# Value and gate columns in one product, second-layer weights split once, and more convolution taps on ScalarE and GpSimd, in a two-layer gated-linear-attention and convolution trunk

## The chip, the cores and the metric

The kernel runs on one core of one Trainium2 chip. The metric is device microseconds of one launch. TensorE (PE) multiplies, VectorE (DVE), ScalarE (ACT) and GpSimd (POOL) work element by element, and SyncE (SP) issues every DMA of this kernel. The language is a tile framework: the program says what is computed in which tile, a scheduler orders the instructions of each engine by priority (by default the order of the program) on a simulated time line, and it hands out buffers and semaphores. An instruction moved ahead with `high_priority(offset=n)` is treated as if it stood n instructions earlier.

## The reference, cut to what matters

The input x has 2048 tokens of 1024 channels. All arithmetic is float32.

```python
h = rmsnorm(x, norm_w[0])                       # layer 0: gated linear attention, 4 heads
q, k, v, z, g_lr = split(h @ gla_w_in)          # 512, 512, 1024, 1024, 16 columns
log_a = log_sigmoid(g_lr @ w_g2 + b_g) / 16
o = gla_chunked(q * 128**-0.5, k, v, log_a)     # chunks of 64 tokens, a state per head runs over chunks
o = o * rsqrt(mean(o * o) + EPS) * gn_w         # per head of 256 value columns
x = x + (o * silu(z)) @ gla_w_out

h = rmsnorm(x, norm_w[1])                       # layer 1: convolution module
a, gl, z = split(h @ conv_w_in)                 # 1024 columns each
u = causal_depthwise_conv(a * sigmoid(gl), dw_w, 31 taps) + dw_b
u = silu(layernorm(u, ln_w, ln_b))
x = x + (u * silu(z)) @ conv_w_out
out = rmsnorm(x, final_norm_w)
```

## The kernel before, in words

**Products.** TensorE works in float32r, a rounded form. To keep float32's accuracy every operand is split into a high part (the rounded copy) and a low part (the rest), and each product is three matmuls: high by high, high by low, low by high (`mm3`, L139 to L145). The splitting is one copy on ScalarE and one subtraction on VectorE or GpSimd for each tile.

**Weights.** All weights lie in DRAM as 32 units of 1 MB (`wall`): 1024 rows by 256 columns, as 128 partitions by 8 row blocks. Units 0 to 11 are the heads of the first layer (for each head: query and key columns, value columns, z columns), 12 to 15 its output projection, 16 to 23 and 24 to 27 the second layer's input (a with gl, and z), 28 to 31 its output. `order` lists the units as they are used; the 4 output units of the second layer come four times, and every other unit twice, once for each half of the tokens. `load_unit` (L110 to L130) brings a unit in two parts of 512 KB through two raw buffers `wr`; for each part ScalarE writes `wh` (L124) and GpSimd writes `wl` (L125; VectorE for the first two units). Two units are kept, the one in use and the next.

**Layer 0.** The tokens go in two halves of 1024, each as two blocks of 512. For each head, `qk` makes query and key for a block feature-major (128 weight columns against 512 tokens, `proj_f`); `values` makes the value rows, 128 tokens at a time against 256 columns of weights (`proj_t`); then `head` goes over the 8 token tiles: the z columns of a tile (again `proj_t` with 256 columns), and the three stages of `core` (scores, mixing with the state, turning), which are issued one token tile apart. In head 0 the values are put into the banks `pb`, so that they can be made while query and key of the block wait in the banks `mm` for the decay factors of `gate`. The output projection `out1` goes over pairs of units; under each pair over both blocks; under each block over 4 channel tiles. After the first block of the second pair it starts the next half (`ahead`: `start_block` with its loads of x, `prep_x`, and the gate's low-rank product `gate_low`, whose small weights `wgs` stay in a tile of their own).

**Layer 1.** `in2` goes over the 12 input units of each half in the order of `SCHED`. A unit of kind u gives one channel tile of a times sigmoid(gl) (`glu`), and its convolution is queued as background work (`bg`): even and odd outputs come from three chains of 16, 15 and 16 taps on VectorE (L634 to L642), of which the first taps of two chains go to ScalarE (products, L620 and L622) and GpSimd (sums, L624); `SIDES` says how many, for each half and channel tile. `pump` issues background work after each piece of TensorE's work. Three `u` tiles are there, so a channel tile waits for the convolution three tiles before it. `layernorm` follows as background work, then `out2`, the output projection, the residual sum and the last normalisation (sum of squares on VectorE, L851).

## Time and profile before

| | us |
|---|---|
| median of 3 runs | 1691.66 (1691.0 to 1695.15) |
| span of the profiled execution, first to last instruction | 1691.3 |
| TensorE busy in it | 1617.2 |
| VectorE busy | 1015.6 |
| GpSimd busy | 936.0 |
| ScalarE busy | 742.2 |

The span and the median differ by 0.4 us, so that the sum over the profile can be read as the time. A busy time is the time in which at least one instruction of the engine runs; matmuls overlap one another, so TensorE is counted busy for a short while after its last one has started.

### The profile page before, as it was taken

How to read it: one execution, taken by the hardware profiler on the slowest of the kernel's cores; microseconds unless marked ns; L12 is line 12 of the kernel's file. 1: busy time of each engine (PE TensorE's matmuls, PEld its weight loads, DVE VectorE, ACT ScalarE, POOL GpSimd, SP SyncE). 2: the span in 40 equal slices, each digit the busy share in tenths (PEclk: the TensorE clock that was granted, in tenths of full speed). 3: DMA queues.
4: the chain of work that ended last, by engine and by line, in shares of the span. 5: the costliest groups of instructions: out<-in, count | busy, mean ns of one | idle time of the engine just before them, and what ended most of it. 6: DMA issues, size and time to landing. Idle time of an engine off the chain costs nothing.

```text
span 1691.3 us, 23564 instructions
## 1 busy us (share of the span) xinstructions
PE 1617.2 (96%) x9028; PEld 1413.4 (84%) x9028; DVE 1015.6 (60%) x1473; ACT 742.2 (44%) x1254; POOL 936.0 (55%) x795
## 2 busy tenths in 40 slices
PE   8999999999999999999999999998999999997887
PEld 6989998988889999999888887876777778776687
DVE  7423232342334323226153999989799999987865
ACT  6645252343466444325232544544462554434432
POOL 4444343334745342424433999983788997465553
PEclk9999999999999999999999999999999999998998
DMA  5021111244511121204461111225127122632743
GB/s 188 30 78 57 63 51 57 76 130 139 164 34 55 58 72 42 75 33 132 132 196 46 63 50 57 85 80 154 38 69 238 61 68 94 206 125 88 235 176 124
DMA packets 74015, 165.68 MB, mean 98 GB/s; under 512 B 7760, under 2 KB 16464, under 8 KB 73904
## 3 DMA queue, kind: packets, MB, share of 16 engines
q1 hardware_dynamic: 73904, 164.19, 29.9%
q8 instruction: 70, 1.15, 0.3%
q14 instruction: 41, 0.34, 0.1%
HBM read 128.51 MB, written 35.65 MB: 97 GB/s over the span
## 4 chain that ended last, share of the span: by engine, by line
PE 62%; DVE 16%; POOL 7%; DMA 6%; issue 4%; ACT 3%; SPq 0%; POOLq 0%; DVEq 0%; ACTq 0%
PE mm L144 52%; DVE pb L638 6%; PE pb L144 3%; DVE al L190 2%; DMA wr<-in_wall_dram 2%; PE pb L388 1%; POOL wl L125 1%; PE pb L390 1%; POOL convB L624 1%; DVE S L713 1%; PE pm L379 1%; POOL convA L624 1%; DVE d L734 1%; POOL b L736 1%; DVE pb L642 1%
## 5 line engine op out<-in xcount | busy, mean ns | idle before, releaser
L144 PE MATMUL mm<-ah,wh 128*128 128x512 f32 (+1 forms) x1600 | 599.1, 389 | 43.2 <-DVE u L761 10.7
L144 PE MATMUL mm<-al,wh 128*128 128x512 f32 (+1 forms) x1600 | 594.6, 387 | 1.7 <-DVE al L190 1.7
L144 PE MATMUL mm<-ah,wl 128*128 128x512 f32 (+1 forms) x1600 | 592.9, 387 | 2.3 <-POOL wl L125 2.3
L125 POOL TENSOR_TENSOR wl<-wr,wh 128x1024 fp32r<-128x1024 f32 x140 | 358.5, 2575 | 195.2 <-ACT wh L124 190.3
L144 PEld LDWEIGHTS mm<-ah,wh 128*128 128x128 f32 x1600 | 304.0, 191 | 109.0 <-DVE u L761 13.1
L144 PEld LDWEIGHTS mm<-ah,wl 128*128 128x128 f32 x1600 | 303.3, 191 | 62.4 <-POOL wl L125 4.2
L144 PEld LDWEIGHTS mm<-al,wh 128*128 128x128 f32 x1600 | 303.9, 191 | 59.7 <-DVE al L190 2.6
L144 PE MATMUL mm<-wh,ah 128*128 128x256 f32 x896 | 259.2, 289 | 0.0
L144 PE MATMUL mm<-wh,al 128*128 128x256 f32 x896 | 254.6, 284 | 0.0
L144 PE MATMUL mm<-wl,ah 128*128 128x256 f32 x896 | 254.2, 284 | 0.0
L124 ACT ACTIVATE wh<-wr 128x1024 fp32r<-128x1024 f32 x144 | 145.3, 1050 | 109.0 <-PE mm L144 78.9
L638 DVE SCALAR_TENSOR_TENSOR pb<-u,C,pb 128x512 f32<-128x512 f32 x252 | 183.8, 747 | 0.5
L638 DVE SCALAR_TENSOR_TENSOR pb<-u,dwc,pb 128x512 f32<-128x512 f32 x240 | 179.4, 748 | 1.6
L144 PEld LDWEIGHTS mm<-wl,ah 128*128 128x128 f32 x896 | 171.4, 191 | 0.4
L144 PEld LDWEIGHTS mm<-wh,ah 128*128 128x128 f32 x896 | 171.3, 191 | 0.4
L144 PEld LDWEIGHTS mm<-wh,al 128*128 128x128 f32 x896 | 171.3, 191 | 0.0
L622 ACT ACTIVATE prod<-u,C 128x512 f32<-128x512 f32 x148 | 105.6, 721 | 137.6 <-POOL convA L624 78.5
L624 POOL TENSOR_TENSOR convA<-convA,prod 128x512 f32<-128x512 f32 x74 | 99.5, 1344 | 6.6 <-ACT prod L622 3.0
L624 POOL TENSOR_TENSOR convB<-convB,prod 128x512 f32<-128x512 f32 x74 | 99.6, 1346 | 3.9 <-ACT convB L620 0.7
L397 DVE SCALAR_TENSOR_TENSOR S<-S,dec,pb 128x256 f32<-128x256 f32 x56 | 26.8, 479 | 95.4 <-PE pb L144 95.3
L401 POOL TENSOR_TENSOR ss<-ss,e 128x1 f32<-128x1 f32 x64 | 13.3, 208 | 124.5 <-ACT g L400 124.5
L523 DVE TENSOR_TENSOR Q<-mm,Q 128x512 f32<-128x512 f32 x32 | 22.0, 688 | 92.7 <-PE mm L144 78.9
(205 smaller groups left out, 2245.3 us busy)
## 6 DMA issues: line engine op xcount, KB each, us to landing
wr<-in_wall_dram SPq DMA_DIRECT2D x144, 512.0 KB, 4.1
raw<-in_xT_dram SPq DMA_DIRECT2D x32, 256.0 KB, 3.8
Q<-in_xT_dram SPq DMA_DIRECT2D x32, 256.0 KB, 3.2
x_scratch<-Q SPq DMA_DIRECT2D x32, 256.0 KB, 3.2
sz_scratch<-t SPq DMA_DIRECT2D x32, 256.0 KB, 2.3
b<-sz_scratch SPq DMA_DIRECT2D x32, 256.0 KB, 3.8
g_scratch<-st SPq DMA_DIRECT2D x48, 128.0 KB, 1.9
raw<-g_scratch SPq DMA_DIRECT2D x24, 256.0 KB, 3.7
```

The costliest lines, as they stand in the source:

```text
L124: act.activation(wh[:, ks, :], raw, AF.Copy)
L125: (dve if i < 2 else pool).tensor_tensor(wl[:, ks, :], raw, wh[:, ks, :].bitcast(F32), ALU.subtract)
L144: pe.matmul(ps, s, m, start=(i == 0), stop=(i == 3 * n - 1))
L190: dve.tensor_tensor(lo, src, hi.bitcast(F32), ALU.subtract)
L379: pe.matmul(s_ps[:, 0:192], ki[:, js], Q[:, j].rearrange("p s c -> p (s c)"), start=True, stop=True)
L388: pe.matmul(o_ps, Q[:, j, 0:2].rearrange("p s c -> p (s c)"), S[h], start=True, stop=False)
L390: pe.matmul(o_ps, x, y, start=first and n == 0, stop=n == 2)
L397: dve.scalar_tensor_tensor(S[h], S[h], dec[:, j:j + 1], kv, ALU.mult, ALU.add)
L523: dve.tensor_tensor(xr, ps, xr, ALU.add)
L622: act.activation(p, src, AF.Copy, scale=w)
L624: pool.tensor_tensor(acc, acc, p, ALU.add)
L638: dve.scalar_tensor_tensor(dstm, src, w, ps, ALU.mult, ALU.add)
```

## The change: what it does, and the diff

- The value and z columns of a head become one product of 512 columns. Their weights lie in two units of 512 rows by 512 columns, and both must be there before a token tile is finished. Values are made tile by tile beside the stages of `core`, in the banks `mm`, in head 0 too.
- The first layer has three places for units (`wh0` to `wh2`, `wl0` to `wl2`), the second two.
- `out1` goes over blocks outside and units inside, so that each of its units is loaded and split twice in each half, and `ahead` is issued after the first block.
- The gate's split weights are written to DRAM once and read back, for each later block, into one of the two raw buffers `wr`. The tag "raw" has 4 buffers, not 5.
- `presplit`: in heads 1 to 3 of both halves, beside the token tiles, the 16 units of the second layer are loaded in 64 pieces of 128 by 512, split (ScalarE, GpSimd), and written to DRAM as high and low parts. In the second layer a unit is then four loads of 512 KB, with no work on ScalarE or GpSimd.
- `SIDES` grows: the taps of ScalarE and GpSimd are 127 for each of two chains, not 90. There are 4 product buffers, not 2, and 6 `t2` tiles, not 4.
- In `out2` the sums of squares of three of the four blocks go from VectorE to GpSimd.

Lines that a part only takes away, with the bodies that stand above, are left out here.

```diff
+UW = 2048
...
-SIDES = ((1, 7, 7, 7, 7, 5, 9, 7),
-         (1, 5, 3, 5, 9, 7, 6, 4))
+SIDES = ((3, 9, 10, 10, 10, 8, 10, 10),
+         (3, 7, 6, 7, 11, 9, 8, 6))
...
+    wsd = tc.dram_tile((16, 2, P, UW), F32, name="ws_scratch")
...
-    wp = ctx.enter_context(tc.tile_pool(name="wp", bufs=2))
+    wp = ctx.enter_context(tc.tile_pool(name="wp", bufs=1))
...
+    half = [(3 * h + j, (2, 0, 1)[j]) for h in range(HEADS) for j in range(3)]
+    half[1:3] = [(1, 1), (2, 0)]
+    half += [(12 + j, c) for j, c in enumerate((2, 0, 1, 2))]
+    half += [(12 + j, c) for j, c in enumerate((0, 2, 1, 0))]
+    order = half * 2
...
+    order += [(u, (n + 1) % 2) for n, u in enumerate(units)]
...
+        u, place = order[i]
+        wpool = wq if place == 2 else wp
+        wh = wpool.tile([P, UW], F32R, name=f"wh{place}")
+        wl = wpool.tile([P, UW], F32R, name=f"wl{place}")
+        wstate["ready"].append((u, place, wh, wl))
+        if u >= 16:
+            for s in range(2):
+                cs = slice(s * UW // 2, (s + 1) * UW // 2)
+                for n, t in enumerate((wh, wl)):
+                    sp.dma_start(out=t[:, cs].bitcast(F32), in_=wsd[u - 16, n, :, cs])
+            return None
...
+    def prefetch(n):
+        while len(wstate["ready"]) < n and wstate["next"] < len(order):
+            if order[wstate["next"]][1] in [u[1] for u in wstate["ready"]]:
+                return
+            load_unit()
...
-    BUFS = {"raw": 5, "tmp": 3, "E": 2, "Ei": 2, "ki": 2, "kd": 1, "st": 4}
+    BUFS = {"raw": 4, "tmp": 3, "E": 2, "Ei": 2, "ki": 2, "kd": 1, "st": 4}
...
+    def gate_weights(first):
+        t = wq.tile([P, UW // 2], F32R, name="wr", bufs=2)
+        wgs = t.rearrange("p (k c) -> p k c", c=P)
+        if not first:
+            sp.dma_start(out=t.bitcast(F32), in_=wgd)
+            return wgs
...
+    pieces = [(u, c) for u in range(16) for c in range(4)]
+
+    def presplit():
+        if not pieces:
+            return
+        u, c = pieces.pop(0)
+        cs = slice(c * NB, (c + 1) * NB)
+        lo, hi = t2("raw"), s2.tile([P, NB], F32R, name="raw", bufs=BUFS["raw"])
+        sp.dma_start(out=lo, in_=wall[16 + u][:, cs])
+        act.activation(hi, lo, AF.Copy)
+        pool.tensor_tensor(lo, lo, hi.bitcast(F32), ALU.subtract)
+        for n, t in enumerate((hi.bitcast(F32), lo)):
+            sp.dma_start(out=wsd[u, n, :, cs], in_=t)
...
+    def values(hf, i, w, a_b):
+        ps = mm_bank()
+        proj_t(ps, w, a_b, i % 4)
+        q = hf * 8 + i
+        vh, vl = (l1p.tile([P, DV], F32R, name=n, bufs=3) for n in ("vh", "vl"))
+        act.activation(vh, ps[:, 0:DV], AF.Copy, scale=r2[:, q:q + 1])
+        dve.scalar_tensor_tensor(vl, ps[:, 0:DV], r2[:, q:q + 1], vh.bitcast(F32), ALU.mult, ALU.subtract)
+        sz = l1p.tile([P, DV], F32, name="sz", bufs=3)
+        act.activation(sz, ps[:, DV:2 * DV], AF.Silu, scale=rt[:, q:q + 1])
+        return (vh, vl), sz
...
+        def tokens(i, w):
+            v, sz = values(hf, i, w, a[i // 4])
+            todo.append(core(hf, h, i, v, sz, qkb[i // 4], sink))
             todo[i][0]()
             if i >= 1:
                 todo[i - 1][1]()
             if i >= 2:
                 todo[i - 2][2]()
+            if h > 0:
+                for _ in range(2 if i in (1, 3, 5) else 1):
+                    presplit()
+        w = next_unit(base, 3)
+        if h == 0:
+            qkb.append(qk(h, w, a[0], EEs[0]))
+            wv = next_wide(base + 1, 2)
+            for i in range(4):
+                tokens(i, wv)
+            start_block(hf, 1, a, EEs, g3s)
+            qkb.append(qk(h, w, a[1], EEs[1]))
+            prefetch(1)
+        else:
+            for b in range(2):
+                run_late(1 if b == 0 else 0)
+                qkb.append(qk(h, w, a[b], EEs[b]))
+            wv = next_wide(base + 1, 3)
+            for i in range(4):
+                tokens(i, wv)
...
-        offset = 0 if hf == b == 0 else 200
+        offset = 200 if hf == 1 else 0
...
+            wgs = first_wgs if hf == b == 0 else gate_weights(False)
...
-        for pair in range(2):
-            ws = [next_unit(12 + 2 * pair), next_unit(13 + 2 * pair)]
-            for b in range(2):
-                t0 = hf * TH + b * NB
-                for ch in range(4 * pair, 4 * pair + 4):
+        for b in range(2):
+            t0 = hf * TH + b * NB
+            acc = l1p.tile([P, NB], F32, name="acc", bufs=2)
+            for u in range(4):
+                w = next_unit(12 + u, 3)
+                for ch in (2 * u, 2 * u + 1):
...
+            if b == 0:
+                ahead()
...
-    s2 = l2.enter_context(tc.tile_pool(name="s2b", bufs=4, reuse_waits="tile"))
+    s2 = l2.enter_context(tc.tile_pool(name="s2b", bufs=6, reuse_waits="tile"))
...
-                p = acc if m == 0 else l2p.tile([P, NB], F32, name="prod", bufs=2)
+                p = acc if m == 0 else l2p.tile([P, NB], F32, name="prod", bufs=4)
...
-                            dve.tensor_tensor(acc, acc, sq, ALU.add)
+                            (dve if ns > 1 else pool).tensor_tensor(acc, acc, sq, ALU.add)
...
+        vz = np.concatenate([w1[:, 1024 + h * 256:1024 + (h + 1) * 256], w1[:, 2048 + h * 256:2048 + (h + 1) * 256]], 1)
+        units += [vz[:512], vz[512:]]
```

## Rows read from the trace of the kernel before

**Rows 1.** The page: busy time of each engine, and one DMA issue.

```profile
PE 1617.2 (96%) x9028; PEld 1413.4 (84%) x9028; DVE 1015.6 (60%) x1473; ACT 742.2 (44%) x1254; POOL 936.0 (55%) x795
...
wr<-in_wall_dram SPq DMA_DIRECT2D x144, 512.0 KB, 4.1
```

**Rows 2.** Windows: busy us (instructions) of each engine by stage; columns in first line.

```profile
core 0: us, PE busy (x) PEld busy (x) DVE busy (x) ACT busy (x) POOL busy (x), PEclk, DMA share, GB/s
0.00:50.00 50.00, 40.67 (x216) 34.42 (x217) 36.59 (x47) 32.56 (x51) 22.70 (x33) 1.00 0.51 159
50.00:425.00 375.00, 374.14 (x2490) 346.20 (x2489) 120.60 (x238) 160.36 (x320) 144.68 (x173) 1.00 0.25 78
425.00:525.00 100.00, 96.89 (x581) 86.85 (x581) 41.28 (x56) 57.19 (x83) 59.66 (x46) 0.97 0.27 87
525.00:1000.00 475.00, 474.54 (x2847) 425.34 (x2846) 206.82 (x348) 189.04 (x361) 214.62 (x224) 1.00 0.25 81
1000.00:1475.00 475.00, 449.00 (x1936) 365.78 (x1935) 454.26 (x590) 222.87 (x316) 384.22 (x267) 0.98 0.31 102
1475.00:1577.00 102.00, 86.27 (x360) 68.05 (x358) 84.88 (x95) 41.51 (x62) 56.16 (x26) 0.93 0.36 119
1577.00:1692.00 115.00, 95.68 (x607) 86.81 (x607) 71.21 (x103) 38.62 (x65) 54.00 (x30) 0.91 0.52 179
```

**Rows 3.** The chain that ended last: start us, us, what, merged count.

```profile
144.25 14.39 PE mm L144 x120
...
924.60 76.20 PE mm L144 x336
```

**Rows 4.** Groups by line and form: count | busy us, mean ns | idle before.

```profile
L144 PE MATMUL mm<-ah,wh 128*128 128x512 f32 x1472 | 567.2, 398 | 39.1 <-DVE u L761 10.7 <-DVE u L845 7.5 <-ACT t L757 7.4
...
L125 POOL TENSOR_TENSOR wl<-wr,wh 128x1024 fp32r<-128x1024 f32 x140 | 358.5, 2575 | 195.2 <-ACT wh L124 190.3 <-DMA wr<-in_wall_dram 4.9
...
L144 PE MATMUL mm<-wh,ah 128*128 128x256 f32 x896 | 259.2, 289 | 0.0
...
L638 DVE SCALAR_TENSOR_TENSOR pb<-u,C,pb 128x512 f32<-128x512 f32 x252 | 183.8, 747 | 0.5
...
L124 ACT ACTIVATE wh<-wr 128x1024 fp32r<-128x1024 f32 x144 | 145.3, 1050 | 109.0 <-PE mm L144 78.9 <-DMA wr<-in_wall_dram 29.8
L622 ACT ACTIVATE prod<-u,C 128x512 f32<-128x512 f32 x148 | 105.6, 721 | 137.6 <-POOL convA L624 78.5 <-POOL convB L624 59.1
L624 POOL TENSOR_TENSOR convB<-convB,prod 128x512 f32<-128x512 f32 x74 | 99.6, 1346 | 3.9 <-ACT convB L620 0.7
...
L205 POOL TENSOR_TENSOR acc<-acc,kTl 128x512 f32<-128x512 f32 x28 | 38.2, 1366 | 59.9 <-ACT kTl L526 59.5
...
L144 PE MATMUL pb<-wh,ah 128*128 128x256 f32 x128 | 37.4, 294 | 1.3 <-DVE vl L438 1.3
...
L851 DVE TENSOR_TENSOR acc<-acc,t 128x512 f32<-128x512 f32 x21 | 22.7, 1081 | 6.3 <-ACT t L849 6.1
```

**Rows 5.** Timeline of ACT near the start: start us, us, what, count.

```profile
47.02 0.63 ACT L322 ACTIVATE E<-Ei 128x512 f32<-128x512 f32 x1 [0.82 <-DVE Ei L320]
```

**Rows 6.** Timeline of PE near the start.

```profile
27.54 0.40 PE L144 MATMUL pb<-wh,ah 128*128 128x256 f32 x2
```

**Rows 7.** Timeline of SP at the first half's output projection.

```profile
351.66 6.59 SPq L269 DMA_DIRECT2D raw<-in_xT_dram  x5
```

**Rows 8.** Waits from 925 to 1480 us: total, times, longest.

```profile
PE mm L144 <- DVE u L761: 10.7, 5, 3.2
```

**Rows 9.** Line 642: duration ns, minimum/median/maximum.

```profile
L642 DVE SCALAR_TENSOR_TENSOR pb<-u,C,convB x16: 746/1478/2891, 926.6 to 1454.2; 128x512 f32<-128x512 f32 x16
```

**Rows 10.** Timeline of DVE from 1104 us.

```profile
1109.18 2.87 DVE L642 SCALAR_TENSOR_TENSOR pb<-u,C,convB 128x512 f32<-128x512 f32 x1 [5.21 <-POOL convB L624]
```

**Rows 11.** Timeline of POOL from 1104 us.

```profile
1109.10 5.17 POOL L125 TENSOR_TENSOR wl<-wr,wh 128x1024 fp32r<-128x1024 f32 x2
```

**Rows 12.** Windows: five us of the last stage, columns as in rows 2.

```profile
1585.00:1590.00 5.00, 5.00 (x31) 4.41 (x30) 1.38 (x2) 1.97 (x4) 0.90 (x2) 1.00 1.04 396
```

More of the change, by code (lines that the diff above doesn't have):

```diff
@@ L103 @@
              U[:3] + Z[:1] + U[3:6] + Z[1:2] + U[6:] + Z[2:]]
-    order = list(range(0, 16)) * 2
+    half = [(3 * h + j, (2, 0, 1)[j]) for h in range(HEADS) for j in range(3)]
[3 more added lines that the diff above has]
+    order = half * 2
+    units = []
     for sched in SCHED:
-        order += [16 + j if s == "u" else 24 + j for s, j in sched]
-    order += list(range(28, 32)) * 4
+        units += [16 + j if s == "u" else 24 + j for s, j in sched]
+    units += list(range(28, 32)) * 4
+    order += [(u, (n + 1) % 2) for n, u in enumerate(units)]
     wstate = {"next": 0, "ready": []}
@@ L130, in load_unit, with pop_unit, next_unit, next_wide @@
         return part
-    def next_unit(expect):
-        while len(wstate["ready"]) < 2 and wstate["next"] < len(order):
+    def prefetch(n):
+        while len(wstate["ready"]) < n and wstate["next"] < len(order):
+            if order[wstate["next"]][1] in [u[1] for u in wstate["ready"]]:
+                return
             load_unit()
-        u, wh, wl = wstate["ready"].pop(0)
+    def pop_unit(expect):
+        u, place, wh, wl = wstate["ready"].pop(0)
         assert u == expect, (u, expect)
         return wh, wl
+    def next_unit(expect, ahead=2):
+        prefetch(ahead)
+        return [w.rearrange("p (k c) -> p k c", c=256) for w in pop_unit(expect)]
+    def next_wide(expect, ahead):
+        prefetch(ahead)
+        w = []
+        for s in range(2):
+            hl = [t.rearrange("p (k c) -> p k c", c=2 * DV) for t in pop_unit(expect + s)]
+            w += [(hl[0][:, k], hl[1][:, k]) for k in range(KT // 2)]
+        return w
     def mm3(ps, terms):
@@ L152, in proj_t @@
     def proj_t(ps, w, a, j):
-        wh, wl = w
         s = slice(j * P, (j + 1) * P)
-        mm3(ps, [(a[k][0][:, s], a[k][1][:, s], wh[:, k, :], wl[:, k, :]) for k in range(KT)])
+        mm3(ps, [(a[k][0][:, s], a[k][1][:, s], w[k][0], w[k][1]) for k in range(KT)])
     def act_pair():
@@ L244, in load_small @@
             dve.tensor_tensor(wgv[:, :, r, 1, :], wgr, wgv[:, :, r, 0, :].bitcast(F32), ALU.subtract)
+        sp.dma_start(out=wgd, in_=t.bitcast(F32))
+        return wgs
     def load_small2():
@@ L428, in core @@
         return scores, mix, turn
-    def values(hf, h, w, a_b, b):
-        vs = []
-        for i in range(4 * b, 4 * b + 4):
-            ps = (b_bank() if h == 0 else mm_bank())[:, 0:DV]
-            proj_t(ps, w, a_b, i % 4)
-            vh, vl = (l1p.tile([P, DV], F32R, name=n, bufs=8) for n in ("vh", "vl"))
-            rr = r2[:, hf * 8 + i:hf * 8 + i + 1]
-            act.activation(vh, ps, AF.Copy, scale=rr)
-            dve.scalar_tensor_tensor(vl, ps, rr, vh.bitcast(F32), ALU.mult, ALU.subtract)
-            vs.append((vh, vl))
-        return vs
+    def values(hf, i, w, a_b):
[8 more added lines that the diff above has]
+        return (vh, vl), sz
@@ L465, in head @@
[L465 to L473 removed]
+        qkb, nxt, todo = [], None, []
+        sink = {"stage": stage}
+        def tokens(i, w):
+            v, sz = values(hf, i, w, a[i // 4])
+            todo.append(core(hf, h, i, v, sz, qkb[i // 4], sink))
@@ L478, in head @@
                 todo[i - 2][2]()
+            if h > 0:
[17 more added lines that the diff above has]
+                tokens(i, wv)
+        if h < HEADS - 1:
+            nxt = gate(h + 1, g3s)
+        for i in range(4, 8):
+            tokens(i, wv)
         late.extend([todo[7][1], todo[6][2], todo[7][2]])
@@ L827, in load_x @@
                 else:
[L828 removed]
+                    t = l2p.tile([P, 1, NB], F32, name="prod", bufs=4)
                     xs.append(t[:, 0])
@@ L968 @@
     units += [wo2[:, j * 256:(j + 1) * 256] for j in range(4)]
-    wall = np.stack([u.reshape(KT, P, 256).transpose(1, 0, 2).reshape(P, KT * 256) for u in units])
+    wall = np.stack([u.reshape(-1, P, u.shape[1]).transpose(1, 0, 2).reshape(P, UW) for u in units])
     def cols(v):
```

74 lines of the change are left out of this document (17 added, 57 removed).

## The prediction

> **What bounds the kernel now.** I read the page's busy times first: TensorE is busy 1617.2 of 1691.3 us, the others at most 60% [rows 1]. Then the windows by stage [rows 2], since a share over the whole span hides two regimes. From 50 to 425 and from 525 to 1000 us TensorE loses 0.9 and 0.5 us: the first layer, and the start of the second, is a gapless stream of matmuls, and only fewer or cheaper matmuls shorten it. From 1000 us on the stream has holes: 26.0, 15.7 and 19.3 us in the last three stages, with VectorE busy 454.3 of 475 us in the first of them. Two smaller holes are the start (9.3 us in the first 50) and the change of halves (3.1 us in 425 to 525).
>
> Idle time understates the loss, because a matmul counts as busy after the next could have started, and because the granted clock is 0.91 to 0.98 in these stages [rows 2], a mean of its two levels, 2.4 and 1.2 GHz, of which the lower follows holes. So I take the price of a matmul from the chain of waits: 120 of 256 columns in 14.39 us are 119.9 ns each, 336 of 512 columns in 76.20 us are 226.8 ns [rows 3]. At that price the 1936 matmuls between 1000 and 1475 us need 439 us, so 36 of 475 are lost; the 360 between 1475 and 1577 us need 82, so 20 of 102 are lost. The last stage mixes both widths, and I keep its idle time, 19, of which some 7 are the tail after the last product.
>
> Why the second layer has holes: TensorE waits for VectorE's product `u` (five waits, 10.7 us, the longest entry of the waits there [rows 8]). VectorE is late because it is nearly full, and because of GpSimd: the same instruction of line 642 takes 0.75 us at its shortest, 1.48 at the median and 2.89 at its longest [rows 9]. The 2.87 us one runs beside two of GpSimd's weight subtractions of 5.17 us together [rows 10, 11]; a VectorE instruction with two operands in SBUF is held while GpSimd works.
>
> **The change part by part.**
>
> *Value and z columns together.* Three kinds of matmul of 256 columns, 896 + 128 of each [rows 4], are 3072; they become 1536 of 512 columns. Each pair costs 2 x 119.9 - 226.8 = 13.0 ns less, in all 20 us, in stages without holes, so that all of it is on the path: **-20**. The Trainium skill, TensorE: Matmul & The Clock Gate, section Back-to-back issue gap, gives a warm gap of N / 2.4 + 2.5 ns, which would be 109.2 and 215.8 ns, 2.5 ns a pair and 4 us in all. Here the two measured gaps differ by 106.9 ns for 256 columns, which agrees with its 106.7, but leave 13 ns a matmul and not 2.5; the measurement decides, and the sum goes by it.
>
> *Start.* Now TensorE has the values to do while query and key hold two of the three banks `mm` until the decay factors come: values start at 27.5 us in banks `pb`, the factors at 47.0 us [rows 5, 6]. Afterwards only one `mm` bank is left for tokens in these 19.5 us; a tile needs 24 x 226.8 ns = 5.4 us and then its readout, and needs two units instead of one, while the gate's weights hold one of the two raw buffers until the low-rank product is done. Two tiles (10.9 us) fit at best: **+8**. Bounds: 0 if a third fits and the loads come early, +15 if only one does.
>
> *Change of halves.* `ahead` now has a whole block of `out1` (8 x 24 x 226.8 ns = 43.5 us) to prepare the next half, where it had half of one, and the second block has four token tiles more of cover. The hole there, 3.1 us idle at a clock of 0.97 [rows 2], mostly closes: **-3**. Against it: the first loads of the next half go out at 351.66 us [rows 7], long before they are used, as soon as a buffer is free. The gate's weights will do the same and keep one of the two raw buffers until their product. A part costs 4.1 us of load, 1.05 on ScalarE and 2.58 on GpSimd [rows 1, 4], 7.7 in all; a unit takes 7.7 us through two buffers and 15.5 through one, and `out1` uses one every 10.9 us. While the buffer is held each unit can lose 4.6 us; the third place holds units made before. I take no loss, and keep +18 (four units) as a bound.
>
> *Output projection by blocks.* 8 units more are split, 16 parts, 41 us on GpSimd and 17 on ScalarE, beside a stage that TensorE fills with 10.9 us a unit: 0.
>
> *Splitting the second layer once.* 64 pieces, each a load, a ScalarE copy, a GpSimd subtraction of 1.37 us (the nearest row of that size, 128x512 from SBUF [rows 4]) and two stores: 87 us of GpSimd over six heads, 48 MB of DMA. GpSimd was busy 144.7 of 375 us there and DMA 25% [rows 2]; with 41 + 87 us in the whole layer it rises from 39% to about 56%. All three DMAs stand in SP's one queue, where a store waits for GpSimd and a weight load behind it waits too; but a head's next units have the 21.8 us of its query and key as cover, and the stages of a token come one tile (about 7 us) apart. The nearest row: subtractions of 2.58 us already stand in GpSimd's queue in this stage and it lost 0.9 us of 375. **0**, bound +15 where each of the 48 tiles of these heads loses 0.3 us.
>
> *Second-layer stream, 925 to 1475 us.* 24 units leave GpSimd (48 x 2.575 = 124 us) and ScalarE. 74 products (0.72 us) and 74 sums (1.35 us, 99.5 us) come, and VectorE loses 74 taps of 0.75 us, 55 us. In 1000 to 1475 us that takes VectorE from 454 to about 406 us against TensorE's 439, before counting that the longest hold on it shrinks from 2.6 to 1.35 us. GpSimd stays near 80%. So TensorE becomes the bound. I do not take all 36: a channel tile with 10 taps gives GpSimd 2 x 9 x 1.35 us of sums and some 6 us more, 30 us, against 21.8 us of TensorE's work, so in the run of u units convolutions fall behind and the three `u` tiles fill. I keep a third: **-24**; bounds -36 and 0.
>
> *Last two stages.* 32 subtractions (82 us) go, which hold VectorE there; 21 sums of 1.08 us leave VectorE. Against it each unit is now 2 MB every 10.9 us. A block moves 8 MB of weights and 4 MB of x and output in 43.5 us, 276 GB/s, with 4 MB more of z in the first half; the busiest five us of this stage moved 396 GB/s at a full DMA share [rows 12]. It fits without much to spare, and with two places the load of a unit can't start before the one before the last is done. Of some 39 lost I take back **-13**; bounds -28 and +12.
>
> *Sum.* -20 + 8 - 3 + 0 - 24 - 13 = -52; 1691.3 - 52 = 1639, and with the 0.4 us between span and median 1640 us.
>
> **Rivals.**
>
> *Convolutions stay the bound (1658 us).* The taps given to GpSimd refill what the weights freed, and its sums hold VectorE as the subtractions did. For it: 99.5 of 124 us come back, and 30 us a unit in the run of u units. Against it: shorter holds, VectorE's 55 us. It keeps 30 of the 36 lost: 1640 + 18. Beside it stands the Trainium skill, Advanced Engine Details and Errata, section Mode Summary: GpSimd's instructions and VectorE's two-port ones share a port and block each other. By it moving work to GpSimd is no pure relief; rows 9 to 11 agree.
>
> *DMA becomes the bound of the output stages (1674 us).* For it: 276 GB/s on average in bursts of four loads of 512 KB, one queue, z loads behind them. Against it: 396 GB/s was moved. If 12 MB take 49 us (246 GB/s) instead of 43.5, four blocks lose 21 us and the 13 saved are gone: 1640 + 34.
>
> *The second layer's holes close wholly (1618 us).* Another 12 us in the stream and 10 in the last stages.
>
> *Raw buffers starve the first layer (1700 us, slower).* If one of the two raw buffers is held through both `out1`s, by the gate's weights or by loads queued in SP behind stores of pieces, a unit takes 15.5 us against 10.9: 4.6 us for 13 or more of the 16 units, 60 us. It decides from a part time of 5.45 us on one buffer, which the 7.7 us exceed; against it stand the third place and that the gate's product needs the buffer only until the next block's x is prepared.
>
> *The join saves little (1656 us).* If the 13 ns belong to something that joining keeps, 4 of the 20 us remain; the two rows of 3 speak against it.
>
> **How the numbers follow.** Forecast 1640 (its own spread 1626 to 1654): 0.50. Convolution bound: 0.19. Wholly closed: 0.12. DMA bound: 0.11. Raw buffers: 0.06. Small join: 0.02. The range 1612 to 1674 holds the first three cases and the edge of the fourth, and leaves the slower one and the far ends of the unknown costs out. A measurement of this kernel can tell about 0.3% (5 us) from no change. Faster by more: all but the raw-buffer case and a part of the DMA case that adds start and head losses, 0.90; within 0.3%: 0.04; slower: 0.06.
>
> **What would show it.** Token-major matmuls of 512 columns at 226.8 ns; TensorE idle below 1 us in the heads of both halves; a hole of some 17 us in the first 50; none at the change of halves; VectorE's share in the second layer's stream under 90% and line 642 nearer to 0.75 us; weight loads of the last stages landing within 10.9 us. The prediction is wrong if TensorE waits for `wl` or `wr` in the first layer, if the stream of the second still loses 30 us, or if TensorE waits for weight DMAs after it.

## The result, and the profile after

The changed kernel takes 1759.17 us (1757.27 to 1761.12, 4 runs) against 1693.4 for the kernel before on the same chip: a ratio of 1.040, 95% interval 1.037 to 1.042. The forecast was 1640 us and the range 1612 to 1674. Unless a run says otherwise, a time below is a median, and the interval beside it is that of its ratio to the kernel before, timed beside it.

The profiled executions differ by 68.0 us of span (1691.3 and 1759.3). The page of after, against [rows 1]: the matmuls are 1536 fewer, TensorE's busy time is not lower.

```profile
PE 1628.1 (93%) x7492; PEld 1339.5 (76%) x7492; DVE 944.0 (54%) x1378; ACT 785.8 (45%) x1343; POOL 974.1 (55%) x890
...
wh<-ws_scratch SPq DMA_DIRECT2D x80, 512.0 KB, 6.5
```

The windows of after with the cuts of [rows 2]; the stages now end later, so that the first rows are to be compared and the later ones hold other work too.

```profile
core 0: us, PE busy (x) PEld busy (x) DVE busy (x) ACT busy (x) POOL busy (x), PEclk, DMA share, GB/s
0.00:50.00 50.00, 30.91 (x107) 21.40 (x108) 36.20 (x39) 32.97 (x50) 28.34 (x33) 0.89 0.67 209
50.00:425.00 375.00, 349.76 (x1642) 290.04 (x1641) 116.86 (x234) 181.09 (x348) 175.40 (x198) 0.96 0.40 130
425.00:525.00 100.00, 95.59 (x428) 77.96 (x427) 41.73 (x42) 49.09 (x70) 79.19 (x51) 0.98 0.58 190
525.00:1000.00 475.00, 446.64 (x2062) 367.95 (x2061) 155.41 (x271) 201.09 (x381) 204.62 (x216) 0.97 0.42 134
1000.00:1475.00 475.00, 448.38 (x1947) 364.61 (x1946) 418.81 (x535) 232.66 (x346) 383.39 (x315) 0.98 0.40 133
1475.00:1577.00 102.00, 100.41 (x432) 80.84 (x431) 92.69 (x127) 43.43 (x69) 50.50 (x37) 0.99 0.65 229
```

In the first layer TensorE is now idle 19 us in the first 50 (9 before), 25 us from 50 to 425 (1 before) and 28 us from 525 to 1000 (under 1 before). The row of before from 1000 us [rows 2] begins 98.3 us behind its first product `u` of the second layer. The same 475 us of after, counted from its own first `u`:

```profile
1077.90:1552.90 475.00, 448.25 (x1936) 363.89 (x1935) 420.82 (x546) 223.25 (x332) 358.90 (x289) 0.98 0.44 148
```

Both stretches hold 1936 matmuls. VectorE has fallen from 454 to 421 us, where 406 was forecast, and nothing came of it.

To split the span between the layers I use that first `u`: its start is the end of the first layer's matmuls and one unit's work. Before it is 901.7 us. The group in after (duration ns minimum/median/maximum, first and last start):

```profile
L818 DVE TENSOR_TENSOR u<-mm,t x32: 1026/1066/1109, 979.6 to 1490.6; 128x512 f32<-128x512 f32 x32
```

So the first layer is 77.9 us longer, the rest (1759.3 - 979.6 = 779.7 against 789.6) only 9.9 shorter. "First u" is that start in each table below, "rest" the span less it.

**Where one hole of the first layer comes from.** ScalarE, GpSimd and TensorE of after around 95 us (start us, us, line, [idle before, and its releaser]):

```profile
92.83 0.63 ACT L412 ACTIVATE raw<-raw 128x512 fp32r<-128x512 f32 x1 [2.84 <-DMA raw<-in_wall_dram]
97.79 0.63 ACT L412 ACTIVATE raw<-raw 128x512 fp32r<-128x512 f32 x1 [4.34 <-DMA raw<-in_wall_dram]
98.33 1.99 ACT L141 ACTIVATE wh<-wr 128x1024 fp32r<-128x1024 f32 x2
102.68 0.63 ACT L412 ACTIVATE raw<-raw 128x512 fp32r<-128x512 f32 x1 [2.37 <-DMA raw<-in_wall_dram]
104.59 0.63 ACT L412 ACTIVATE raw<-raw 128x512 fp32r<-128x512 f32 x1 [1.28 <-DMA raw<-in_wall_dram]
105.13 0.58 ACT L340 ACTIVATE tmp<-pb 96x512 f32<-96x512 f32 x1
106.46 0.63 ACT L344 ACTIVATE g<-tmp 96x512 fp32r<-96x512 f32 x1 [0.75 <-DVE tmp L342]
```

```profile
93.53 1.26 POOL L413 TENSOR_TENSOR raw<-raw 128x512 f32<-128x512 f32 x1 [2.50 <-ACT raw L412]
94.75 1.02 POOL L202 TENSOR_TENSOR rt<-v,mhalf 128x4 f32<-128x4 f32 x1
```

```profile
95.82 1.16 PE L212 MATMUL pb<-ident,rt 128*128 128x128 f32 x8 [3.21 <-POOL rt L202]
...
97.79 0.63 PE L179 MATMUL mm<-wl,ah 128*128 128x512 f32 x1
98.22 0.63 PE L179 MATMUL mm<-wh,al 128*128 128x512 f32 x1
...
101.16 0.39 PE L179 MATMUL mm<-wl,ah 128*128 128x512 f32 x1
101.39 0.40 PE L179 MATMUL mm<-wh,al 128*128 128x512 f32 x1
...
107.95 0.77 PE L353 MATMUL pb<-g,g2t 96*128 96x512 f32 x1 [6.16 <-DVE g L345]
```

Read it backwards. TensorE waits 3.21 us for `rt`, a tiny operation that stands on GpSimd behind a piece's subtraction (L413), which waited 2.50 us for its ScalarE copy (L412, at 92.83), which waited 2.84 us for the piece's load. Then TensorE waits 6.16 us for `g`: its readout (L340) stands on ScalarE behind three copies of pieces that wait 4.34, 2.37 and 1.28 us for theirs. Neither the readout nor `rt` needs a piece. Over the span, ScalarE's waits for the loads of pieces and GpSimd's waits for their copies are the second and the fourth in the list of all waits (total, times, longest):

```profile
DVE g L460 <- POOL ss L459: 119.2, 52, 9.7
ACT raw L412 <- DMA raw<-in_wall_dram: 119.1, 47, 6.8
...
POOL raw L413 <- ACT raw L412: 93.3, 41, 5.7
```

This stretch, 92 to 111 us, lies in head 0. The pieces are issued in heads 1 to 3 in program order, but nothing ties them there: their loads went out from 34 us.

### The profile page after: what moved, and what is told of

Its sections match the earlier page's. It is cut to its first block, busy times and chain, and to the rows that moved or that the text cites. A ratio compares the mean times of both kernels' runs of the same rounds, so it can differ in the third digit from the quotient of the medians.

```text
span 1759.3 us, 21194 instructions
## 1 busy us (share of the span) xinstructions
PE 1628.1 (93%) x7492; PEld 1339.5 (76%) x7492; DVE 944.0 (54%) x1378; ACT 785.8 (45%) x1343; POOL 974.1 (55%) x890
## 4 chain that ended last, share of the span: by engine, by line
PE 34%; DMA 20%; DVE 15%; POOL 14%; issue 8%; ACT 7%; SPq 1%; POOLq 0%; ACTq 0%; DVEq 0%
PE mm L179 30%; DMA raw<-in_wall_dram 6%; DVE pb L695 6%; POOL convB L681 4%; POOL convA L681 3%; DMA wr<-in_wall_dram 3%; DMA ws_scratch<-raw 3%; POOL wl L142 2%; DMA x_scratch<-Q 2%; DVE d L791 1%; DVE pb L699 1%; ACT raw L412 1%; DMA b<-sz_scratch 1%; PE pb L445 1%; DMA t<-y_scratch 1%
## 5 line engine op out<-in xcount | busy, mean ns | idle before, releaser
L179 PE MATMUL mm<-wh,ah 128*128 128x512 f32 x512 | 209.9, 410 | 16.4 <-ACT sz L496 14.9
L142 POOL TENSOR_TENSOR wl<-wr,wh 128x1024 fp32r<-128x1024 f32 x76 | 187.7, 2481 | 63.1 <-ACT wh L141 55.4
L179 PE MATMUL mm<-wl,ah 128*128 128x512 f32 x512 | 207.1, 404 | 4.6 <-POOL wl L142 2.9
L179 PE MATMUL mm<-wh,al 128*128 128x512 f32 x512 | 206.6, 403 | 0.0
L413 POOL TENSOR_TENSOR raw<-raw 128x512 f32<-128x512 f32 x64 | 83.2, 1304 | 93.8 <-ACT raw L412 93.3
L695 DVE SCALAR_TENSOR_TENSOR pb<-u,C,pb 128x512 f32<-128x512 f32 x178 | 130.1, 746 | 0.5
L179 PEld LDWEIGHTS mm<-wh,ah 128*128 128x128 f32 x512 | 99.3, 194 | 38.4 <-ACT sz L496 16.5
L141 ACT ACTIVATE wh<-wr 128x1024 fp32r<-128x1024 f32 x80 | 82.6, 1055 | 94.0 <-DMA wr<-in_wall_dram 68.1
L179 PEld LDWEIGHTS mm<-wl,ah 128*128 128x128 f32 x512 | 99.5, 194 | 25.3 <-POOL wl L142 3.9
L179 PEld LDWEIGHTS mm<-wh,al 128*128 128x128 f32 x512 | 99.3, 194 | 20.3
L412 ACT ACTIVATE raw<-raw 128x512 fp32r<-128x512 f32 x64 | 40.2, 629 | 129.5 <-DMA raw<-in_wall_dram 119.1
```

The costliest lines, as they stand in the source:

```text
L141: act.activation(wh[:, cs], raw, AF.Copy)
L142: (dve if i < 2 else pool).tensor_tensor(wl[:, cs], raw, wh[:, cs].bitcast(F32), ALU.subtract)
L179: pe.matmul(ps, s, m, start=(i == 0), stop=(i == 3 * n - 1))
L412: act.activation(hi, lo, AF.Copy)
L413: pool.tensor_tensor(lo, lo, hi.bitcast(F32), ALU.subtract)
L695: dve.scalar_tensor_tensor(dstm, src, w, ps, ALU.mult, ALU.add)
```

## The experiments

**Without pieces, and pieces held in place.** In the first run `presplit` is not called, and the second layer loads one stand-in unit again and again and leaves the other 15 out; its traffic stays. In the second each piece is tied to its token.

```diff
-                for _ in range(2 if i in (1, 3, 5) else 1):
-                    presplit()
```

> The changed kernel without the 64 pieces: nothing of the second layer's weights is split beside the first layer; the second layer loads its high and low parts as before from DRAM, but always those of one stand-in unit that is written once after head 3 (so the weights of the second layer are wrong, its traffic is kept). Theory A, the pieces ran in head 0 and not in heads 1 to 3 (loads at 34 to 187 and 515 to 647 us in the trace) and blocked ScalarE, GpSimd and SP there: the first layer ends near 905 us where it ended at 970, and the time is about 1695 us. Rival B, the joined product itself (both units needed, one bank left in head 0, the gate's weights in a raw buffer): little is given back, 1745 us or more.

```diff
+        act.activation(lo[:, 0:1], tie[:, 0:1], AF.Copy)   # tie: this token's sz
         sp.dma_start(out=lo, in_=wall[16 + u][:, cs])
```

> The changed kernel with each piece held to its place: one column of the piece's buffer is first written by ScalarE from the token tile's own silu(z), so that its load can't go out before that tile. All 64 pieces and all their work stay. Theory A (the place in time): most of what leaving them out gives, 1700 to 1715 us. Rival C (the work and the traffic of the pieces cost the same wherever they stand): 1740 us or more. Rival B: 1745 or more.

1701.62 us (1.003 to 1.008) and 1781.67 (1.049 to 1.053). Pieces cost 58 us, and the theory that they cost only because they run too early fell: held, they cost 80.

**Former taps; the changed first layer alone.** In the second run the pieces are left out and the second layer is that of the kernel before, splits included.

```diff
-SIDES = ((3, 9, 10, 10, 10, 8, 10, 10), (3, 7, 6, 7, 11, 9, 8, 6))
+SIDES = ((1, 7, 7, 7, 7, 5, 9, 7), (1, 5, 3, 5, 9, 7, 6, 4))
```

> The changed kernel with the former share of taps for ScalarE and GpSimd (90 instead of 127). The first layer stays as it is. Theory D, VectorE is still what the second layer's stream waits for: 74 taps of 0.75 us go back to it and the time rises by 10 to 40 us, to 1770 to 1800. Rival E, the sums on GpSimd and the waits of ScalarE for them took back what the weights freed: it falls by 5 to 20 us, to 1740 to 1755.

> The changed kernel's first layer without the pieces, and the second layer of the kernel before (weights split at each use, former taps, former buffers, sums of squares on VectorE); the result is the reference's. It shows the joined product and the output projection by blocks alone. Theory A: 20 us less matmul time, 10 to 15 more lost at the start, 3 gained at the change of halves: about 1680 to 1688 us. Rival B: the first layer still ends 60 us or more late, 1740 or more.

1749.52 us (1.030 to 1.036) and 1720.58 (1.013 to 1.018). With the former taps the rest is 758.9 us against 779.7, so the new taps cost 21 us there and not 10: the first layer, whose code is the same in both, has its first `u` 8.7 us later (988.3 and 979.6). So two builds can differ by some 9 us in a stage that no edit touched, and a difference of that size at the first `u` of one build is no finding by itself. The joined first layer is slower than the old one by itself (first `u` at 924.6 against 901.7). For the taps rival E came true; for the joined layer neither of my bounds did.

**Traffic alone and work alone.**

```diff
-        act.activation(hi, lo, AF.Copy)                     # traffic alone
-        pool.tensor_tensor(lo, lo, hi.bitcast(F32), ALU.subtract)
...
-        sp.dma_start(out=lo, in_=wall[16 + u][:, cs])       # work alone
-        act.activation(hi, lo, AF.Copy)
+        act.activation(hi, scanm, AF.Copy)
```

> The kernel after with the pieces' transfers alone: each piece is still loaded and stored twice (48 MB, one raw buffer instead of two), but ScalarE's copy and GpSimd's subtraction are left out, so the second layer multiplies with unsplit weights twice. Theory W (the cost is ScalarE and GpSimd standing in order behind a piece's load): nothing waits for a load any more, the cost goes and the time is near that without pieces, 1700 to 1715 us. Rival T (the cost is the traffic: SP's queue, the DMA engines, late weight loads): 1740 us or more. In between means both. The second layer is that of the kernel after, 784 to 789 us long.

> The kernel after with the pieces' work alone: 64 ScalarE copies and GpSimd subtractions of 128x512 stay in their places, but work on a constant that is always there; no piece is loaded or stored, and the second layer loads one stand-in unit as the run without pieces did. Theory W (waiting for loads): 1700 to 1715 us. Rival P (the 87 us of GpSimd and the copies themselves delay the tokens' chains): 1730 us or more. If this run and the one with the traffic alone both come near 1702, the cost is neither the work nor the traffic, but the work standing behind the traffic.

1712.48 us (1.010 to 1.014) and 1722.50 (1.016 to 1.021). At the first `u` of the profiled runs traffic costs 11.4 us, work 20.7, both together 54.2: some 22 us exist only when the work and the traffic are there together. Theory W, waiting for loads, speaks of that part and not of the rest.

**Staggered; held work; each engine's part.** The staggered run ties a piece's load to a token and its copy to the next token. The other three hold the work on constants: both engines, GpSimd only, ScalarE only.

```diff
         lo = t2("raw")
+        act.activation(lo[:, 0:1], tie[:, 0:1], AF.Copy)    # this token
         sp.dma_start(out=lo, in_=...)
...
+        act.activation(hi[:, 0:1], tie[:, 0:1], AF.Copy)    # the next token
         act.activation(hi, lo, AF.Copy)
```

> The kernel after with the pieces held beside the tokens of heads 1 to 3 and taken in two steps: ScalarE first writes one column from the token's z values, so that a piece's load starts with its token (as in the held run, 1781.7 us), and its copy, subtraction and stores are tied in the same way to the next token, some 7 us later, when the load has landed. Same work, same traffic, same heads. Theory W (the copy and the subtraction stand in order and wait for the piece's own load): heads 1 to 3, which took 84, 96 and 84 us in the held run and 70, 82 and 84 us without pieces, come back to within 4 us of the latter, 1705 to 1730 us. Rival P (the work and the traffic themselves, wherever and however they stand): 1750 us or more.

> The kernel after with the work of the pieces alone (copy and subtraction on a constant tile, no transfers, second layer from a stand-in unit, as in the run with the work alone, 1722.5 us), but each piece tied by one written column to its token of heads 1 to 3. In the run without the tie they crowded into head 0, where GpSimd was busy 54.6 of 80 us instead of 24.4. Theory E (place: the work costs because it runs early, in head 0, where the decay factors are late): 1700 to 1710 us, heads 1 to 3 as without pieces. Rival P (the work itself delays tokens in any head): 1718 us or more.

> The run with the held work alone (1730.2 us) with GpSimd's part only: each token of heads 1 to 3 gives GpSimd one 128x512 subtraction on a constant tile (tied by a one-column one on the token's z values), ScalarE gets nothing, nothing is loaded or stored. Without any piece: 1701.6 us. If GpSimd's queue is what delays the tokens' chains: 1718 us or more. If ScalarE's is: 1700 to 1709.

> The run with the held work alone (1730.2 us) with ScalarE's part only: one copy of 128x512 of a constant tile for each piece, tied by a one-column copy to the token's z values; no GpSimd subtraction, no transfers. If ScalarE's queue is what delays the tokens' chains: 1715 us or more. If GpSimd's is: 1700 to 1709. Where both parts alone stay under 1710, they cost only together.

| run | us | ratio, interval | first u | over no pieces | heads 0 | heads 1 to 3 | `out1` |
|---|---|---|---|---|---|---|---|
| no pieces | 1701.62 | 1.003 to 1.008 | 925.4 | | | | |
| after | 1759.17 | 1.037 to 1.042 | 979.6 | 54.2 | 63 | -6 | -2 |
| traffic alone | 1712.48 | 1.010 to 1.014 | 936.8 | 11.4 | 7 | 2 | 3 |
| work alone | 1722.50 | 1.016 to 1.021 | 946.1 | 20.7 | 28 | -6 | 1 |
| held | 1781.67 | 1.049 to 1.053 | 1004.0 | 78.6 | -4 | 58 | 23 |
| held, staggered | 1735.48 | 1.022 to 1.027 | 958.3 | 32.9 | -2 | 11 | 24 |
| held, work on constants | 1730.25 | 1.019 to 1.025 | 949.8 | 24.4 | -1 | 12 | 16 |
| of that GpSimd's part | 1716.68 | 1.010 to 1.017 | 941.2 | 15.8 | 1 | -1 | 17 |
| of that ScalarE's part | 1715.64 | 1.010 to 1.016 | 939.9 | 14.5 | -2 | 4 | 13 |

The last three columns say where in the profiled run the excess over no pieces lies, both halves added. Head 0 ends with its last readout of z, heads 1 to 3 end with that of head 3, and `out1` ends with its last residual sum. TensorE can be some us ahead of such a mark or behind it (after has 39 matmuls, 9 us, done ahead at the end of the first head 0), so neighbouring columns share a few us.

After pays in the two heads 0, where nothing but the scheduler had put the pieces. Held, heads 1 to 3 pay 58 us; staggered, each copy a token after its load, they pay 11. The same work and traffic cost 46 us less, and all of it in these heads. TensorE's waits from 130 to 525 us, held and then staggered (L461 and L469 are the same line):

```profile
PE pb L179 <- DVE g L461: 19.2, 11, 4.5
PE pb L446 <- DVE S L455: 4.4, 2, 3.5
```

```profile
...
PE pm L479 <- DVE g L469: 2.4, 1, 2.4
...
PE pb L179 <- DVE g L469: 2.3, 3, 1.0
```

That is the chain of a token: its sum stands in one of two banks `pb` until ScalarE squares it, GpSimd takes the power (`ss`) and VectorE scales it (`g`). Whatever stands in ScalarE's or GpSimd's queue ahead of it holds the bank.

What is left in the staggered run, 33 us, is for the larger part something else. All five held runs lose 13 to 24 us in `out1`, the three without any load of a piece too. `out1` brings the heads' outputs back into tiles of the tag "raw", and the pieces take tiles of that tag. Without pieces its twelve loads in the first half go out during the heads, from 126 to 363 us; in each held run all twelve go out at 369 us or later. No pieces, and then GpSimd's part alone (issues of those loads, and a window with the columns of [rows 2]):

```profile
332.49 5.92 SPq L558 DMA_DIRECT2D raw<-g_scratch  x6
...
370.00:380.00 10.00, 10.00 (x48) 8.28 (x47) 3.94 (x9) 4.30 (x8) 7.17 (x8) 1.00 0.71 239
```

```profile
371.01 1.37 SPq L558 DMA_DIRECT2D raw<-g_scratch  x3
...
370.00:380.00 10.00, 5.18 (x21) 3.48 (x20) 4.40 (x7) 6.14 (x15) 8.79 (x11) 0.81 0.73 237
```

In both of these runs head 3 of the first half ends at 371.7 us; from there the one with GpSimd's part takes 13.5 us longer to the end of `out1`. So its 16 us are no price of the subtractions in the heads, which lose nothing by them; the copies alone cost the heads 4 us, and both together 12. That the pieces hold the tiles of `out1` until the last token is my reading of the program and of these issues; tiles of their own were not tried on this kernel. The bounds that I gave these four runs went by the whole time and did not see this: 1735.48 and 1716.68 lie between theirs, and 1730.25 and 1715.64 fall on the side of a delay in the heads, though half of their excess or more is not there.

**The start.** On the run without pieces: gate weights in two idle stage tiles and the old priority of the second block; then the first two tokens in the banks `pb`.

```diff
+            t = s2.tile([P, NB], F32R, name="st", bufs=BUFS["st"])
...
-        offset = 200 if hf == 1 else 0
+        offset = 0 if hf == b == 0 else 200
```

> The kernel after without pieces (second layer from a stand-in unit, as in the run without pieces, 1701.6 us), with two changes at the start: the gate's weights of the first block lie in two stage tiles that are not in use yet, so that both raw buffers are free for units 1 and 2, and the second block of the first half is prepared with the priority that it had in the kernel before. Theory R (one raw buffer, and the late second block): the hole from 30 to 50 us falls from 15 us to 8 or less, that from 90 to 110 us (3 idle, gate factors of block 1 at 105 us) goes, in all 1686 to 1693. Rival O (one bank of the product left until the decay factors come, whatever the buffers): the hole at 30 to 50 us stays above 10 us and the time is 1695 to 1702.

```diff
-        ps = mm_bank()
+        ps = b_bank() if hf == 0 and h == 0 and i < 2 else mm_bank()
```

> The kernel after without pieces (stand-in unit, 1701.6 us), with the first two tokens of the first head in the two pb banks, where the kernel before had its values, instead of in the one mm bank left. Two raw buffers more did nothing for the hole from 30 to 50 us (15.9 us, waits for the readout of z). Theory B (the bank): the hole falls to 8 us or less and the time to 1688 to 1695. Rival U (units 1 and 2 come too late whatever the bank): hole above 12 us, 1698 to 1704.

1708.30 us (1.007 to 1.014) and 1700.05 (1.004 to 1.008), against 1701.62. Windows of before, of the run without pieces, of the first and of the second:

```profile
30.00:50.00 20.00, 19.05 (x133) 17.68 (x132) 12.24 (x18) 12.32 (x19) 10.73 (x11) 1.00 0.08 26
50.00:130.00 80.00, 79.14 (x528) 72.96 (x527) 28.18 (x54) 43.33 (x78) 35.59 (x46) 1.00 0.18 57
```

```profile
30.00:50.00 20.00, 9.96 (x25) 5.91 (x26) 13.74 (x10) 12.89 (x20) 14.82 (x8) 0.67 0.41 133
50.00:130.00 80.00, 76.73 (x357) 62.90 (x357) 27.82 (x51) 38.34 (x68) 24.43 (x31) 0.98 0.11 34
```

```profile
30.00:50.00 20.00, 13.45 (x51) 10.18 (x49) 7.34 (x8) 10.43 (x16) 14.34 (x11) 0.83 0.28 95
50.00:130.00 80.00, 70.05 (x325) 57.45 (x324) 20.88 (x41) 39.65 (x63) 23.70 (x30) 0.96 0.11 37
```

```profile
30.00:50.00 20.00, 17.02 (x75) 13.19 (x74) 12.28 (x10) 12.53 (x17) 14.26 (x9) 1.00 0.42 134
50.00:130.00 80.00, 70.55 (x312) 58.19 (x313) 22.49 (x46) 37.05 (x63) 24.30 (x30) 0.91 0.13 38
```

The bank does make the hole from 30 to 50 us (10.0 us idle fall to 3.0), but the idle time turns up behind it: from 30 to 130 us it is 1.8 us before and 13.3, 16.5 and 12.4 in the three. Both fixes missed the times that I gave them, and the first, which changes buffers and priority at once, is worse than no fix (first `u` 931.9 against 925.4). So neither gives the start back. My reading, not tested: in the new order tokens with their whole chains stand before the second block's preparation, which the eight value tiles covered before.

**The taps without pieces.** Same edit of `SIDES`, on the run without pieces.

> The kernel after without pieces (stand-in unit, 1701.6 us) and with the former numbers of taps on ScalarE and GpSimd; only the taps differ from the run without pieces. Theory (the new taps cost what loading split weights gains): the second layer falls from 784 to 764 to 770 us, in all 1681 to 1688. Rival (in the run with pieces and former taps the gain of 10 us came from elsewhere): the second layer stays within 4 us of 784, 1697 to 1704.

1681.12 us (0.991 to 0.996), as the theory said. Rest: 757.6 us against 774.4, at an unchanged first layer (first `u` 923.5 and 925.4). The window from 1000 to 1475 us with the new taps and with the former:

```profile
1000.00:1475.00 475.00, 450.76 (x1958) 367.10 (x1956) 424.29 (x544) 230.84 (x343) 377.15 (x305) 0.99 0.42 138
```

```profile
1000.00:1475.00 475.00, 457.99 (x1981) 374.54 (x1980) 447.16 (x609) 188.92 (x278) 299.61 (x240) 0.98 0.43 143
```

VectorE is 23 us busier with the former taps, and TensorE gets more done. What VectorE's last tap of a chain (line 698 in both) waited for before it, us and times, new taps and then former:

```profile
  POOL convB L680: 23.7, 7
  POOL convA L680: 11.9, 3
```

```profile
  POOL convA L680: 10.5, 1
  POOL convB L680: 1.0, 2
```

The page's shares of the chain that ended last, again new taps and then former:

```profile
PE 47%; POOL 14%; DMA 12%; DVE 12%; issue 8%; ACT 6%; SPq 1%; POOLq 0%; DVEq 0%; ACTq 0%
```

```profile
PE 57%; DVE 19%; DMA 8%; issue 5%; ACT 5%; POOL 4%; SPq 0%; POOLq 0%; DVEq 0%; ACTq 0%
```

**Towards a better version.** All start from the kernel before. First: each second-layer unit is stored when it is first split, later uses load it. Second: only the four units of the last projection are split ahead, one piece beside each block of the first half's `out1`, staggered. Third: the same 16 pieces in tiles that are idle there, eight in each half.

```diff
+                for t, d in zip((wh, wl), ws):                      # first
+                    sp.dma_start(out=d[:, ks, :], in_=t[:, ks, :].bitcast(F32))
...
+                    presplit(xr)                                    # second
...
+            lo = t2("ki")                                           # third; hi in "kd"
+                    presplit(xr, pair == 0)
```

> The kernel before, with one thing added: a unit of the second layer that is split for the first time is also stored split (32 MB of stores), and its 24 later uses load the two halves instead of splitting again. The first layer is untouched (893 us), so nothing is paid there. Theory G (GpSimd's subtractions are what holds the second layer; loading split weights gained some 20 to 30 us with the former taps): the second half of the stream and three of the four output blocks gain, 1693 - 15 to 20 = 1673 to 1680 us. Rival D (transfers and the stores' places in SP's queue eat it): 1688 to 1700 us.

> The kernel before, with 16 pieces only: the four units of the second output projection, which are used four times each, are split once beside the 16 blocks of the first half's first output projection, a load per block and its copy and subtraction one block (5.4 us) later, and loaded split afterwards. Tokens of the heads are left alone. Theory: in that stage only VectorE's sums free TensorE's banks, so the pieces cost at most 3 us, and the last two stages gain what they gained with split weights and the former taps (17 and 6 us): 1693 - 20 = 1670 to 1678 us. Rival: the pieces delay the weight units or the next half's start: 1688 us or more.

> The kernel before with the same 16 pieces of the second output projection's units as the run before this one (1686.0 us), but in tiles that nothing else uses in that stage (the ones of the scaled keys) instead of the raw tiles, and eight each beside the first two groups of four channel blocks of both first output projections, before the next block's x is prepared. In the run before, the first output projection and the change of halves took 19 us longer, because the loads of the next half's x waited for raw tiles that pieces held, while the last two stages gained 23 us. Theory (the shared tiles and the late pieces cost the 19 us): both projections stay within 3 us of before, 1666 to 1675 us. Rival (the pieces' work and traffic cost it, in whichever tiles): 1680 us or more.

| run | us | ratio, interval | first u | rest |
|---|---|---|---|---|
| before | 1691 to 1694 | | 901.7 | 789.6 |
| stored at first use | 1686.91 | 0.996 to 0.998 | 912.6 (46 matmuls ahead) | 768.2 |
| output units only | 1686.04 | 0.994 to 0.998 | 922.0 | 763.2 |
| output units, own tiles | 1682.20 | 0.992 to 0.996 | 913.4 | 763.3 |

All three beat both kernels by a little, and all three missed the gain that I expected. In the first, 46 more matmuls (10 us) than in before stand ahead of the first `u`, and its first layer ends 6 us earlier; so its later first `u` is no price, and the gain is the whole span's, 10.5 us in the profiled runs. In the other two the rest shortens by 26 us, and the first layer, with the change of halves, pays 20 and 12 of it. Own tiles, with half of the pieces in the other half, give 8.6 us back. Which wait they end is not shown: ScalarE waits for the next half's x 5.4 us in before, 9.7 with shared tiles and 7.7 with own, and with own tiles it waits another 8.3 us for stores out of the one buffer of `kd`. Of the kernels that compute the whole result the last one is the fastest, 0.6% faster than before.

## Why the prediction was wrong, point by point

The terms in the first layer without the pieces were to give -15 us and gave +24 (first `u` 925.4 against 901.7). The pieces were put at 0 and cost 54 there. The rest was to give -37 and gave -10. Together that is the 68 us of the spans.

*Splitting once, 0 with a bound of +15: the step that failed most, 54 us at the first `u`.* Its volumes were right (87 us of GpSimd forecast, 83.2 measured for the 64 subtractions). Two sentences were wrong. "Beside the token tiles of heads 1 to 3" is program order; the loads started at 34 us, and the cost lies in the heads 0. And "stages of a token come one tile apart" was read as slack, while the bank `pb` that a token holds goes through ScalarE's and GpSimd's in-order queues. I compared busy shares, 39% to 56%; a queue whose head waits for a load is not busy, and blocks all the same. The runs split the 54: about 11 traffic alone, 21 work alone, and 22 only with both, each from one build and so good to some 9 us. That these 22 are work standing behind its load is seen in the waits of after and in the 46 us that staggering gave back in the heads.

*Start, +8 with a bound of +15.* Right in kind, but three times the term and beyond its bound. In the run without pieces the last z readout of head 0 ends 23.6 us later than before (136.0 against 112.4), join included, and that is the whole of the 24 us. The bank was the first cause of the hole and not of the loss; I had not priced the cover that the second block's preparation loses. What it would take to restore it was not found.

*Value and z together, -20.* From the chain of after, 63 matmuls in head 2 of the first half:

```profile
255.13 14.44 PE mm L179 x63
```

229.2 ns each (two thirds of them joined ones), 10.6 less than 2 x 119.9 [rows 3]: 16 us over 1536. The Trainium skill's 2.5 ns a matmul (TensorE: Matmul & The Clock Gate, Back-to-back issue gap), by which 4 us would be the estimate, does not fit that row either. Right in mechanism; heads 1 to 3, three quarters of the 16 us, are 5.6 and 3.3 us shorter without pieces than before in the two halves.

*Change of halves -3, `out1` by blocks 0.* Not so: without pieces the two `out1` take 102.7 and 104.2 us where they took 95.4 and 101.6, some 10 us worse. The order by blocks was not tried apart, so the cause stays open.

*Second-layer stream, -24 of 36.* The rival "convolutions stay the bound" (chance 0.19) happened. VectorE's fall was two thirds of the forecast (421 us where 406 was forecast, 454 before); the conclusion that TensorE becomes the bound was wrong. A tap on the side costs VectorE 0.75 us less and puts 1.35 us into a serial chain on GpSimd that VectorE's last tap must wait for: in after line 699 (642 before) waits 25.1 us for `convB`, where it waited 5.2 before. I also expected its duration near 0.75 us, and its median is 1.76, not lower than the 1.48 of before [rows 9]:

```profile
L699 DVE SCALAR_TENSOR_TENSOR pb<-u,C,convB x16: 745/1764/2893, 1012.7 to 1528.5; 128x512 f32<-128x512 f32 x16
```

With the former taps the whole rest gains 789.6 - 757.6 = 32 us from loading split weights (and from the buffers and the moved sums of squares that came with it), near the 37 that I gave both stages; the new taps take 17 to 21 of them back. By the Trainium skill (Advanced Engine Details and Errata, Mode Summary) GpSimd and VectorE's two-port instructions block each other at a shared port, which speaks against such a move. The runs agree in sign, with the former taps faster by 20.5 us. But the waits put it on the chain: without pieces line 698 waits 35.6 us for the two GpSimd chains with the new taps and 11.5 with the former, while its median duration behind `convB`, which a block would stretch, is 1.58 and 1.70.

*Last stages, -13.* Right in size: from the end of the first sum of `out2` to the end 214.2 us instead of 225.4, -11. TensorE waits 7.3 us for weight loads there, one of the signs that I had named, so transfers cost at most that much. The stream before it, from the first `u` to that sum, takes 565 us against 564: the 24 us forecast are all missing there.

*Raw buffers starve the first layer (slower, 0.06).* The sign came true, the mechanism did not: in the whole first layer of after TensorE waits 6.6 us for weight units (1.1 before), all in the first 50 us. It was the one slower rival that I wrote, and the cost sat elsewhere; its sign is luck.

Open: what restores the start; why `out1` by blocks is slower; whether own tiles for the pieces end the loss of the held runs in `out1`; and what part of the differences of a few us comes from the order that the scheduler finds anew for each build (the two builds that differ in the second layer's taps only are 2 us apart at the end of the first head 0, and 8.7 at the first `u`).

## What to carry to other kernels

Before side work is costed at nothing because its engines are half idle, name each instruction of the critical chain that passes through those in-order queues, and ask what the side work waits for when it reaches the head: stagger its copy behind its load, or keep it out of such stretches. Ask too which tiles it takes, and what loads need those tiles next. Program order is no place in time unless data ties it there. And moving work from a nearly full engine to a slacker one buys nothing if it comes back as a serial chain that the full engine waits for.

## What the runs showed of the hardware

A short hole costs twice: after the 3.21 us of waiting at 95.8 us the 512-column matmuls follow each other 0.43 us apart (97.79, 98.22), and 0.23 us apart again from 101 us. The granted clock is 1.00 from 92 to 96 us and 0.50 from 97.8 to 99.0 us, the lower of the two levels (1.2 GHz). In the run without pieces and with one bank the granted clock from 30 to 50 us is 0.67, with the two tokens in the other banks it is 1.00.
